# A fused encoder layer on one core: eight mixer weights split by GpSimd, square roots moved ahead of the last gate's output, and the K, V and Q projections moved in front of the pair jobs

## The chip, the core and the metric

The kernel runs on one NeuronCore of a Trainium2 chip. A core has five engines that run their own instruction queues in order and meet at semaphores: TensorE (PE in the profile; its weight loads are listed apart as PEld), VectorE (DVE), ScalarE (ACT), GpSimd (POOL) and SyncE (SP, which here only issues loads and stores). Operands lie in SBUF; matrix products come out in PSUM, in banks of 128 x 512 fp32. The metric is the device time of one execution in microseconds; the compared numbers are medians of several executions.

## What is computed

One layer of a hybrid encoder for 512 tokens and a model width of 1024, all in fp32: a SwiGLU feed-forward, a mixer, and a second feed-forward. The change lies in the mixer.

```python
u = rms_norm(h, mix_pre_g[l])
q, k, v, xr, xg = jnp.split(u @ w_in[l], splits, axis=-1)
xr = causal_conv(xr, conv_w[l], conv_b[l])
hr = rg_lru(xr, rg_a_w[l], rg_a_b[l], rg_x_w[l], rg_x_b[l], lru_lambda[l])
y_a = (hr * jax.nn.gelu(xg)) @ w_lru_out[l]
y_b = swa_sink_attention(q, k, v, attn_sinks[l], bias) @ w_attn_out[l]
g = jax.nn.sigmoid(u @ w_gate[l] + b_gate[l]).reshape(b, s, N_BRANCHES, d)
merged = g[:, :, 0] * y_a + g[:, :, 1] * y_b
h = h + rms_norm(merged @ w_o[l], mix_post_g[l])
```

`rg_lru` forms, for every channel, two sigmoid gates from small block products, a decay `a`, an input scaled by `sqrt(1 - a^2)`, and the scan `h[t] = a[t] * h[t-1] + input[t]` over the tokens.

## The kernel before, in words

**Split operands.** TensorE multiplies in fp32r, a shortened fp32. Every operand is therefore kept as two parts, a high part (the value copied to fp32r) and a low part (value minus high part), and a product is the sum of three matmuls: high weight by high input, low weight by high input, high weight by low input (lines 218 to 220 for plain units, 487 to 489 for pair jobs). A weight tile of 128 x 1024 is loaded raw by SyncE (`dma_one`, line 140, tile `raw_...`), its high part `whi` is a ScalarE copy (line 173) and its low part `wlo` a VectorE subtraction (line 174). For the keys in `BY_DMA` (line 1376) it goes another way, `split_dma` (line 152): ScalarE makes the high part and a negated copy of it, and an accumulating load issued by GpSimd adds the raw weight from memory to the negated copy. In the kernel before, these are the first four gate weights (`wg` 0 to 3) and, inside the pair jobs, the first split of every job but job 0.

**Units.** `unit(nm, i)` makes one 128-channel strip of a projection for all 512 tokens: 8 x 3 matmuls of 128 x 512 into one PSUM bank. `get` (line 178) hands out a unit's weight, emits the splits of the two weights that follow in the hand-written list `order` (line 96 on), and the raw loads of three more. A split stops at the indices in `paired`, the weights of pair jobs, which are prepared elsewhere.

**The hand-made order.** All engines' instructions are emitted in one program order and each queue keeps it. `later(n, fn, rank)` puts work `n` points ahead; `point()` counts up and emits what is due, lowest rank first. Each unit holds two points (after its 12th and 24th matmul) and each V product one; a pair job has one after each of its products. `point(True)` emits all that is outstanding.

**The mixer's stages before.** Relative to the start of the mixer's point count: four units of `xr` (points 1 to 8); eight units of `wg`, the gates of branch A (points 9 to 24); four V products (25 to 28); four pair jobs for `xg`; two K units; two Q units; then the eight output units of the recurrent branch (`lru`) mixed with the other Q units and the attention steps, and so on. Beside them run the convolution (`CONV_AT`), the recurrent gates (`RG_AT`), the decays (`DECAY_AT`: ScalarE exp and tanh, then three VectorE operations, lines 1047 to 1053), the square roots (`rg_scan`, line 1060, on ScalarE at the points of `SCAN_AT`) and, `SCAN_LAG` points later, the product and the scan on VectorE (lines 1063 and 1064). `gate_out` (line 1107) takes a gate's tanh out of its bank one point after its unit.

**Pair jobs.** `GeluPairs.run` makes `xg` by a fast 2 x 2 block scheme with seven products instead of eight. A job takes two raw weights; its operands are a11/a12 (first raw weight), the sums s1 to s4 (tiles `S`, made by GpSimd, lines 532 to 538) and a22. `prep(m, i)` prepares job m in five steps: 0, the four GpSimd sums; 1, the split of a11/a12; 2 and 3, the splits of the sums; 4, the split of a22. Within job n the steps 1 to 4 of job n+1 are emitted between the products, and at its end step 0 of job n+2 and the raw loads of job n+3. Job 0's steps and job 1's sums come earlier, at the points of `PREP_AT` and `PREP_1`. The seventh product of a job (a22) is made in the next job. After a job come the gelu (ScalarE), the product with the scan's result (line 686) and its split into `yh` and `yl`, the inputs of the `lru` units; four jobs give four pairs of these. The last job is followed by its own seventh product, product and split, and the first `lru` unit reads all four pairs.

**Buffers.** Nearly all SBUF tiles come from one pool of 42 slots of 4 KB a partition (`NSLOT`). A tile takes a slot when it is first used in program order, and its first writer waits until the slot's last reader is done; so SyncE's queue stops at a load whose slot is not yet free. `KS`, the split K of one KV head, fills four slots in all and `QS` one slot for each Q unit.

Of the kernel before, what the change touches and what calls it, by code (L numbers as in the profile page):

```python
# [15 lines left out]
P = 128  # L16
# [35 lines left out]
def hybrid_layer(ctx: ExitStack, tc: tile.TileContext, a: dict, out: bass.AP):  # L52
# [22 lines left out]
    def f32(ap):  # L75
        return ap.bitcast(F32)
# [41 lines left out]
    want("w2a", FT)  # L118
    order += [("xr", i) for i in range(8)]
    order += [("wg", i) for i in range(8)]  # L120
    order += [("wv", 0), ("wv", 1)]
    paired.update(range(len(order), len(order) + 8))
    order += [("xg", i) for i in range(8)]
    order += [("wk", 0), ("wk", 1), ("wq", 0), ("wq", 1)]

    att_units = [("lru", 0), ("wq", 2), ("wq", 3), ("lru", 1), ("wq", 4), ("wq", 5), ("lru", 2), ("lru", 3)]
    att_units += [("wq", 6), ("lru", 4), ("wq", 7), ("lru", 5), ("lru", 6), ("lru", 7)]
# [24 lines left out]
    def split_dma(r, src, shape=(P, D), hi=None):  # L152

        lo = slot(list(shape), F32R, name="wlo")
        if hi is None:
            hi = slot(list(shape), F32R, name="whi")
            act.activation(hi, r, AF.Copy)
        act.activation(lo, r, AF.Copy, scale=-1.0)
        pool.dma_start(out=lo, in_=src, accum_op=ALU.add)
        return hi, lo  # L160

    def split_to(n):
        while st["split"] < min(n, len(order)) and st["split"] not in paired:
            k = st["split"]
            dma_to(k + 1)
            r = raws.pop(k)
            if order[k] in BY_DMA:
                nm, i = order[k]
                pairs[k] = split_dma(r, a[nm][i * P : (i + 1) * P, :])
            else:  # L170
                hi = slot([P, D], F32R, name="whi")
                lo = slot([P, D], F32R, name="wlo")
                act.activation(hi, r, AF.Copy)
                dve.tensor_tensor(out=lo, in0=r, in1=f32(hi), op=ALU.subtract)
                pairs[k] = (hi, lo)
            st["split"] += 1

    def get(nm, i, ahead=2, rawahead=3):

        k = st["get"]  # L180
        assert order[k] == (nm, i), (order[k], nm, i)
        dma_to(k + 1 + ahead)
        split_to(k + 1 + ahead)
        dma_to(st["split"] + rawahead)
        st["get"] += 1
        return pairs.pop(k)
# [5 lines left out]
    def later(n, fn, rank=1):  # L192
        uid[0] += 1
        due.append((now[0] + n, rank, uid[0], fn))
# [297 lines left out]
    class Pairs:  # L492
# [14 lines left out]
        def prep(self, m, i, eng=None):  # L507
            if m >= len(self.jobs) or (m, i) in self.ready:
                return
            self.ready.add((m, i))  # L510
            k = self.k0 + 2 * m
            if i == 0:
                if k not in loaded or k + 1 not in loaded:
                    self.raws(m)
                s12, s34 = slot([P, 2 * QH], name="S12"), slot([P, 2 * QH], name="S34")
                self.w[m] = {"r": (raws.pop(k), raws.pop(k + 1)), "s": (s12, s34)}
            W = self.w[m]
            (ra, rb), (s12, s34) = W["r"], W["s"]
            a11, a12, a21, a22 = ra[:, :QH], ra[:, QH:], rb[:, :QH], rb[:, QH:]

            def both(src, w=2 * QH):
                hi = slot([P, w], F32R, name="whi")
                lo = slot([P, w], F32R, name="wlo")
                split2(hi, lo, src)
                return hi, lo

            def halves(p, a, b):
                W[a] = p[0][:, :QH], p[1][:, :QH]
                W[b] = p[0][:, QH:], p[1][:, QH:]

            def sums34(e):
                e.tensor_tensor(out=s34[:, QH:], in0=a12, in1=s12[:, QH:], op=ALU.subtract)
                e.tensor_tensor(out=s34[:, :QH], in0=a11, in1=a21, op=ALU.subtract)  # L533

            if i == 0:
                e = eng or pool
                e.tensor_tensor(out=s12[:, :QH], in0=a21, in1=a22, op=ALU.add)
                e.tensor_tensor(out=s12[:, QH:], in0=s12[:, :QH], in1=a11, op=ALU.subtract)
                if self.R is None:
                    sums34(e)  # L540
            elif i == 1:
                nm, t_ = order[k]
                p = split_dma(ra, a[nm][t_ * P : (t_ + 1) * P, :]) if nm in BY_DMA and m else both(ra)
                halves(p, "a11", "a12")
            elif i == 2:
                if self.R is not None:
                    sums34(dve)
                halves(both(s12), "s1", "s2")
            elif i == 3:
# [534 lines left out]
    for i, p in enumerate(PREP_AT):  # L1084
        later(p, lambda i=i: pairs_g.prep(0, i), 3)
    later(PREP_1, lambda: pairs_g.prep(1, 0), 3)


    lru, scans = {}, []
# [4 lines left out]
        later(p, lambda i=i: rg_gates(i))  # L1094
    for i in range(8):
        later(DECAY_AT[i], lambda i=i: rg_decay(i), 3)
        later(SCAN_AT[i], lambda i=i: rg_scan(i), 3)
    xr_ps = dict(enumerate(bs))
    for i in range(4, 8):
        xr_ps[i] = unit("xr", i)  # L1100
# [8 lines left out]
    for i in range(8):  # L1109
        ps = unit("wg", i)  # L1110
        later(1, lambda i=i, ps=ps: gate_out(i, ps))

    wv = [get("wv", i) for i in range(2)]
    V2 = [slot([P, 2, N_KV, 2, HD], F32R, name="V") for _ in range(2)]

# [14 lines left out]
        later(1, lambda t=t, o=o: v_out(t, o))  # L1130
        point()

    yh, yl = [], []
    pairs_g.run(scans, yh, yl, lambda: split_to(st["split"] + 1))
    X3 = pairs_g = None

    KS = {}

    def k_out(i, ps):
        ks = {r0: slot([P, 2, SEQ], F32R, name="KS") for r0 in (0, 64)}  # L1140
        for r0, k_ in ks.items():
            act.activation(k_[0:64, 0, :], ps[r0 : r0 + 64, :], AF.Copy)
            act.activation(k_[64:128, 0, :], ps[r0 : r0 + 64, :], AF.Copy)
        for r0, k_ in ks.items():
            dve.tensor_tensor(out=k_[r0 : r0 + 64, 1, :], in0=ps[r0 : r0 + 64, :], in1=f32(k_[r0 : r0 + 64, 0, :]), op=ALU.subtract)
        for r0, k_ in ks.items():
            o0 = 64 - r0
            act.activation(k_[o0 : o0 + 64, 1, :], f32(k_[r0 : r0 + 64, 1, :]), AF.Copy)
            KS[2 * i + r0 // 64] = k_

    for i in range(2):
        ps = unit("wk", i)
        later(1, lambda i=i, ps=ps: k_out(i, ps))
    QS = {}

    def q_out(i, ps):
# [8 lines left out]
    for i in range(2):  # L1165
        ps = unit("wq", i)
        later(1, lambda i=i, ps=ps: q_out(i, ps))

    def ya_out(i, ps):
        m = gz[i // 2][:, i % 2, :]  # L1170
# [194 lines left out]
ATT_LAG = (1, 1, 4, 1, 3, 1)  # L1365
RG_LAG = 2
DECAY_AT = (9, 10, 13, 14, 17, 18, 21, 22)
SCAN_AT = (25, 25, 25, 25, 26, 26, 26, 26)
SCAN_LAG = (1, 1, 2, 2, 2, 2, 3, 5)

T_AT = (3, 4, 5, 6), (4, 5, 6, 7)
PREP_AT = (19, 21, 23, 24, 25)
PREP_1 = 24
NSLOT = 42

BY_DMA = {("wg", i) for i in range(4)} | {"xg"}
RF = 7
RO = 6

# [58 lines left out]
```

## Time and profile before

| quantity | value |
|---|---|
| median of 3 runs | 1147.79 us (1144.2 to 1148.16) |
| profiled execution | 1145.55 us |
| its span on the core | 1142.8 us |
| mean granted TensorE clock | 0.994 |
| TensorE busy | 1122.5 us |
| VectorE busy | 823.7 us |
| ScalarE busy | 628.1 us |
| GpSimd busy | 353.7 us |
| bytes moved | 130.75 MB, mean 114 GB/s |

The span runs from the first to the last instruction of the core; the profiled execution's time is 2.75 us longer. The times of the rows count from the span's start. In the profile `c` is a PSUM bank of the pair jobs, `f` one of a unit, `v` one of V; `S` a tile of sums; `ct`, `cc` a job's results; `xc_t` the tile in which the recurrent branch keeps decay and root; `ig` the scan's tile. A row of instructions reads: start, length, engine, line, operation, output<-input, shape, count, and in brackets the idle time of the engine just before with what ended it. A row of a group reads: line, engine, operation, names and shapes, count, then busy time, mean ns of one, and idle time before. A row of waits reads: engine, line, what it waited for, total us, times, longest. Matmuls overlap, so a row's length is more than the distance to the next start; the distance is the rate.

### The profile page before, as it was taken

How to read it: one execution, taken by the hardware profiler on the slowest of the kernel's cores; microseconds unless marked ns; L12 is line 12 of the kernel's file. 1: busy time of each engine (PE TensorE's matmuls, PEld its weight loads, DVE VectorE, ACT ScalarE, POOL GpSimd, SP SyncE). 2: the span in 40 equal slices, each digit the busy share in tenths (PEclk: the TensorE clock that was granted, in tenths of full speed). 3: DMA queues.
4: the chain of work that ended last, by engine and by line, in shares of the span. 5: the costliest groups of instructions: out<-in, count | busy, mean ns of one | idle time of the engine just before them, and what ended most of it. 6: DMA issues, size and time to landing. Idle time of an engine off the chain costs nothing.

```text
span 1142.8 us, 17893 instructions
## 1 busy us (share of the span) xinstructions
PE 1122.5 (98%) x6973; PEld 1012.7 (89%) x6973; DVE 823.7 (72%) x1224; ACT 628.1 (55%) x1112; POOL 353.7 (31%) x274
## 2 busy tenths in 40 slices
PE   9999999999999999789999999999999999999997
PEld 7899999988889878788888888888999999998886
DVE  5889989796346968966678855767899777975313
ACT  7755565573246698466656653455555555574211
POOL 0043444200002404331466553000865566700000
PEclk9999999999999999899999999999999999999999
DMA  9226553364404651345122223431323332255101
GB/s 348 92 80 152 139 117 111 96 218 148 129 37 166 156 123 54 93 115 180 38 93 93 75 92 129 158 138 38 111 82 105 112 98 88 92 189 177 40 19 55
DMA packets 38725, 130.75 MB, mean 114 GB/s; under 512 B 4704, under 2 KB 6624, under 8 KB 38640
## 3 DMA queue, kind: packets, MB, share of 16 engines
q1 hardware_dynamic: 34128, 114.89, 30.1%
q0 software_dynamic: 4224, 14.20, 6.5%
q8 instruction: 54, 0.88, 0.3%
q10 hardware_dynamic: 288, 0.52, 0.1%
q14 instruction: 31, 0.25, 0.1%
HBM read 120.17 MB, written 7.33 MB: 112 GB/s over the span
## 4 chain that ended last, share of the span: by engine, by line
PE 55%; DMA 1%; DVE 0%; issue 0%; ACT 0%; DVEq 0%
PE c L488 6%; PE c L487 6%; PE c L489 6%; PE f L218 6%; PE f L220 6%; PE f L219 6%; PE acc L238 5%; PE acc L237 5%; PE acc L236 5%; PE pt L1235 1%; PE s L1199 1%; DMA wlo<-in_xg_dram 1%; PE s L1198 1%; PE o L1251 1%; PE o L1252 1%; PE tr L328 0%
## 5 line engine op out<-in xcount | busy, mean ns | idle before, releaser
L488 PE MATMUL c<-uT,wlo 128*128 128x256 f32 x504 | 143.5, 285 | 8.5 <-DMA wlo<-in_xg_dram 8.5
L218 PE MATMUL f<-uT,whi 128*128 128x512 f32 (+1 forms) x408 | 146.7, 360 | 0.0
L488 PE MATMUL c<-Xh,wlo 128*128 128x256 f32 x504 | 143.4, 285 | 2.8 <-DVE wlo L209 2.8
L219 PE MATMUL f<-uT,wlo 128*128 128x512 f32 (+1 forms) x408 | 145.3, 356 | 0.0
L220 PE MATMUL f<-uT,whi 128*128 128x512 f32 (+1 forms) x408 | 145.2, 356 | 0.0
L487 PE MATMUL c<-Xh,whi 128*128 128x256 f32 x504 | 143.2, 284 | 0.0
L489 PE MATMUL c<-uT,whi 128*128 128x256 f32 x504 | 143.2, 284 | 0.0
L487 PE MATMUL c<-uT,whi 128*128 128x256 f32 x504 | 143.0, 284 | 0.0
L236 PE MATMUL acc<-whi,hT 128*128 128x512 f32 x352 | 137.1, 390 | 0.0
L237 PE MATMUL acc<-wlo,hT 128*128 128x512 f32 x352 | 137.0, 389 | 0.0
L238 PE MATMUL acc<-whi,hT 128*128 128x512 f32 x352 | 136.9, 389 | 0.0
L489 PE MATMUL c<-Xl,whi 128*128 128x256 f32 x456 | 129.0, 283 | 0.0
L209 DVE TENSOR_TENSOR wlo<-S,whi 128x1024 fp32r<-128x1024 f32 x84 | 125.2, 1491 | 2.4 <-ACT whi L208 1.4
L488 PEld LDWEIGHTS c<-uT,wlo 128*128 128x128 f32 x504 | 97.3, 193 | 9.1 <-DMA wlo<-in_xg_dram 9.1
L488 PEld LDWEIGHTS c<-Xh,wlo 128*128 128x128 f32 x504 | 97.3, 193 | 3.2 <-DVE wlo L209 3.1
L208 ACT ACTIVATE whi<-S 128x1024 fp32r<-128x1024 f32 x84 | 86.1, 1054 | 22.0 <-DVE S L533 22.0
L487 PEld LDWEIGHTS c<-Xh,whi 128*128 128x128 f32 x504 | 97.3, 193 | 0.3 <-issue 0.3
L489 PEld LDWEIGHTS c<-uT,whi 128*128 128x128 f32 x504 | 97.3, 193 | 0.0
L487 PEld LDWEIGHTS c<-uT,whi 128*128 128x128 f32 x504 | 97.2, 193 | 0.0
L218 PEld LDWEIGHTS f<-uT,whi 128*128 128x128 f32 x408 | 77.1, 189 | 12.0 <-issue 1.4
L489 PEld LDWEIGHTS c<-Xl,whi 128*128 128x128 f32 x456 | 87.5, 192 | 0.0
L220 PEld LDWEIGHTS f<-uT,whi 128*128 128x128 f32 x408 | 77.1, 189 | 11.1
(352 smaller groups left out, 2832.6 us busy)
## 6 DMA issues: line engine op xcount, KB each, us to landing
raw_w2a<-in_w2a_dram SPq DMA_DIRECT2D x22, 512.0 KB, 4.2
raw_w1b<-in_w1b_dram SPq DMA_DIRECT2D x22, 512.0 KB, 4.2
raw_w3b<-in_w3b_dram SPq DMA_DIRECT2D x22, 512.0 KB, 4.2
raw_w2b<-in_w2b_dram SPq DMA_DIRECT2D x22, 512.0 KB, 4.1
raw_w3a<-in_w3a_dram SPq DMA_DIRECT2D x21, 512.0 KB, 4.6
raw_w1a<-in_w1a_dram SPq DMA_DIRECT2D x20, 512.0 KB, 4.4
raw_wg<-in_wg_dram SPq DMA_DIRECT2D x16, 512.0 KB, 4.0
raw_xr<-in_xr_dram SPq DMA_DIRECT2D x8, 512.0 KB, 4.0
```

The lines of the kernel that those rows point to most:

```text
L208: act.activation(hi, src, AF.Copy)
L209: dve.tensor_tensor(out=lo, in0=src, in1=f32(hi), op=ALU.subtract)
L218: pe.matmul(ps[:, c0:c1], wh[:, s], h_, start=k == 0, stop=False)
L219: pe.matmul(ps[:, c0:c1], wl[:, s], h_, start=False, stop=False)
L220: pe.matmul(ps[:, c0:c1], wh[:, s], l_, start=False, stop=k == KT - 1)
L236: pe.matmul(acc[n], x[:, 0, c], wh[:, s], start=first, stop=False)
L237: pe.matmul(acc[n], x[:, 0, c], wl[:, s], start=False, stop=False)
L238: pe.matmul(acc[n], x[:, 1, c], wh[:, s], start=False, stop=last)
L487: pe.matmul(ps, wh[:, s], xh, start=first, stop=False, skip_group_check=True)
L488: pe.matmul(ps, wl[:, s], xh, start=False, stop=False, skip_group_check=True)
L489: pe.matmul(ps, wh[:, s], xl, start=False, stop=k == 3, skip_group_check=True)
L1198: pe.matmul(o, lq, KS[g][:, 0, k0 : k0 + n], start=True, stop=False)
```

## The change

It does four things, in one edit.

1. The list `order` has K ahead of V, and V and Q ahead of `xg`; the code of the K and Q units stands ahead of `pairs_g.run`, with one `point(True)` between. The points are then: gates 9 to 24, K 25 to 28, V 29 to 32, Q 33 to 36, then the pair jobs, then `lru` 0.
2. The new set `BY_POOL` names `wg` 2 to 7 and both K weights: their high part is a GpSimd `tensor_copy` in place of the ScalarE copy; the low part is the VectorE subtraction. `BY_DMA` keeps `wg` 0 and 1 alone, and the pair jobs' step 1 always splits with a ScalarE copy and a VectorE subtraction.
3. All eight square roots are emitted at point 23 (rank 4, the last of what is due there), which is ahead of the last gate's tanh at point 25; the scans follow one by one at points 24 to 31.
4. The first two raw weights of the pair jobs are loaded at point 18 and the next two at point 27 (`RAW_AT`); job 0's steps move to points 22, 27, 29, 31 and 33, job 1's sums to point 30.

```diff
     order += [("wg", i) for i in range(8)]
-    order += [("wv", 0), ("wv", 1)]
+    order += [("wk", 0), ("wk", 1), ("wv", 0), ("wv", 1)]
+    order += [("wq", 0), ("wq", 1)]
     paired.update(range(len(order), len(order) + 8))
     order += [("xg", i) for i in range(8)]
-    order += [("wk", 0), ("wk", 1), ("wq", 0), ("wq", 1)]
...
-                act.activation(hi, r, AF.Copy)
+                if order[k] in BY_POOL:
+                    pool.tensor_copy(hi, r)
+                else:
+                    act.activation(hi, r, AF.Copy)
                 dve.tensor_tensor(out=lo, in0=r, in1=f32(hi), op=ALU.subtract)
...
             elif i == 1:
-                nm, t_ = order[k]
-                p = split_dma(ra, a[nm][t_ * P : (t_ + 1) * P, :]) if nm in BY_DMA and m else both(ra)
-                halves(p, "a11", "a12")
+                halves(both(ra), "a11", "a12")
...
     later(PREP_1, lambda: pairs_g.prep(1, 0), 3)
+    for n, p in enumerate(RAW_AT):
+        later(p, lambda n=n: [dma_one(pairs_g.k0 + 2 * n + j) for j in range(2)], 3)
...
-        later(SCAN_AT[i], lambda i=i: rg_scan(i), 3)
+        later(SCAN_AT[i], lambda i=i: rg_scan(i), 4)
...
-SCAN_AT = (25, 25, 25, 25, 26, 26, 26, 26)
-SCAN_LAG = (1, 1, 2, 2, 2, 2, 3, 5)
+SCAN_AT = (23,) * 8
+SCAN_LAG = (1, 2, 3, 4, 5, 6, 7, 8)
...
-PREP_AT = (19, 21, 23, 24, 25)
-PREP_1 = 24
+RAW_AT = (18, 27)
+PREP_AT = (22, 27, 29, 31, 33)
+PREP_1 = 30
...
-BY_DMA = {("wg", i) for i in range(4)} | {"xg"}
+BY_DMA = {("wg", i) for i in range(2)}
+
+BY_POOL = {("wg", i) for i in range(2, 8)} | {("wk", 0), ("wk", 1)}
```

The functions `k_out` (a K strip out of its bank into two `KS` tiles: four ScalarE copies, two VectorE subtractions, two more ScalarE copies) and `q_out` (two ScalarE copies, two VectorE operations) are moved as they are.

More of the change, by code (lines that the diff above doesn't have):

```diff
@@ L1111, in hybrid_layer, with k_out @@
         later(1, lambda i=i, ps=ps: gate_out(i, ps))
+    KS = {}
+    def k_out(i, ps):
+        ks = {r0: slot([P, 2, SEQ], F32R, name="KS") for r0 in (0, 64)}
+        for r0, k_ in ks.items():
+            act.activation(k_[0:64, 0, :], ps[r0 : r0 + 64, :], AF.Copy)
+            act.activation(k_[64:128, 0, :], ps[r0 : r0 + 64, :], AF.Copy)
+        for r0, k_ in ks.items():
+            dve.tensor_tensor(out=k_[r0 : r0 + 64, 1, :], in0=ps[r0 : r0 + 64, :], in1=f32(k_[r0 : r0 + 64, 0, :]), op=ALU.subtract)
+        for r0, k_ in ks.items():
+            o0 = 64 - r0
+            act.activation(k_[o0 : o0 + 64, 1, :], f32(k_[r0 : r0 + 64, 1, :]), AF.Copy)
+            KS[2 * i + r0 // 64] = k_
+    for i in range(2):
+        ps = unit("wk", i)
+        later(1, lambda i=i, ps=ps: k_out(i, ps))
     wv = [get("wv", i) for i in range(2)]
@@ L1131, in hybrid_layer @@
         point()
[L1133 to L1153, printed above, removed]
     QS = {}
@@ L1167, in hybrid_layer @@
         later(1, lambda i=i, ps=ps: q_out(i, ps))
+    yh, yl = [], []
+    point(True)
+    pairs_g.run(scans, yh, yl, lambda: split_to(st["split"] + 1))
+    X3 = pairs_g = None
     def ya_out(i, ps):
```

## The prediction

> **What bounds the kernel now.** The page's head and first part come first, then the waits of TensorE (line waited for, total, times, longest).
>
> ```profile
> span 1142.8 us, 17893 instructions
> ...
> PE 1122.5 (98%) x6973; PEld 1012.7 (89%) x6973; DVE 823.7 (72%) x1224; ACT 628.1 (55%) x1112; POOL 353.7 (31%) x274
> ```
>
> ```profile
> PE c L488 <- DMA wlo<-in_xg_dram: 8.5, 3, 4.0
> PE c L488 <- DVE wlo L209: 2.8, 1, 2.8
> PE w L722 <- DVE tiny L728: 1.4, 1, 1.4
> PE c L487 <- ACT ct L672: 0.5, 1, 0.5
> ```
>
> TensorE sets the end: it is busy for 98%, and apart from the start its only waits, 8.5 + 2.8 + 0.5 = 11.8 us, all carry the name c, the banks of the pair jobs. The next two views are busy times by stretch (the columns after the length are PE, PEld, DVE, ACT, POOL, then granted clock and DMA), and TensorE's own order of time.
>
> ```profile
> 402.00:450.87 48.87, 48.87 (x230) 38.88 (x229) 37.08 (x50) 47.50 (x65) 8.64 (x6) 1.00 0.40 94
> 450.87:462.59 11.72, 11.72 (x99) 11.68 (x97) 11.61 (x11) 8.20 (x15) 6.54 (x4) 1.00 0.05 4
> 462.59:518.56 55.97, 44.28 (x339) 43.18 (x338) 42.94 (x44) 29.34 (x48) 17.64 (x11) 0.91 0.48 130
> 470.00:480.00 10.00, 4.44 (x25) 3.94 (x23) 9.90 (x8) 0.50 (x2) 6.26 (x4) 0.70 0.55 152
> ```
>
> ```profile
> 450.62 0.39 PE L219 MATMUL f<-uT,wlo 128*128 128x512 f32 x1
> 450.85 0.39 PE L220 MATMUL f<-uT,whi 128*128 128x512 f32 x1
> ...
> 462.59 0.28 PE L487 MATMUL c<-uT,whi 128*128 128x256 f32 x1
> 462.71 0.28 PE L488 MATMUL c<-uT,wlo 128*128 128x256 f32 x1
> ...
> 475.55 0.58 PE L488 MATMUL c<-uT,wlo 128*128 128x256 f32 x1 [4.04 <-DMA wlo<-in_xg_dram]
> 475.92 0.41 PE L489 MATMUL c<-uT,whi 128*128 128x256 f32 x1
> 476.14 0.41 PE L487 MATMUL c<-uT,whi 128*128 128x256 f32 x1
> ...
> 518.40 0.40 PE L218 MATMUL f<-uT,whi 128*128 128x512 f32 x1
> ```
>
> Pair matmuls start every 0.12 us, but after the 4.04 us wait every 0.21 us, while the granted clock of that stretch reads 0.70. The four jobs hold 28 products of 12 matmuls: 336 x 0.12 = 40.3 us. They take 518.40 - 462.59 = 55.8 us. So **15.5 us** are lost here, 11.8 as waits and about 3.7 to the slower clock and restarts. That is the most that can be won; before and after this stretch TensorE has no gap. A 128x512 matmul takes 0.23 us, so a unit of 24 takes 5.5 us.
>
> **The parts.** *High and low parts of the pair weights.* For jobs 1 to 3 the low part of a11/a12 is now made by ScalarE (a negated copy) and an accumulating load issued by GpSimd.
>
> ```profile
> 468.24 0.88 POOL L159 DMA_DIRECT2D wlo<-in_xg_dram  x1 [10.45 <-ACT ct L660]
> ```
>
> ```profile
> raw_xg<-in_xg_dram SPq DMA_DIRECT2D x8, 512.0 KB, 3.6
> ...
> wlo<-in_xg_dram POOLq DMA_DIRECT2D x3, 512.0 KB, 7.3
> ```
>
> Job 0's seventh product comes only in job 1, so it lasts 6 x 12 x 0.12 = 8.6 us, and this load, issued 5.6 us into it, lands 7.3 us later: 4.3 us past the start of job 1, which is the wait seen. The change makes the low part by one subtraction on VectorE after the same high-part copy. The 8.5 us go, and since the code has no such load for xg any more, that part cannot fail to happen; VectorE gains 3 x 1.22 us (row L174 below), ScalarE loses three copies.
>
> *The copies.*
>
> ```profile
> L208 ACT ACTIVATE whi<-S 128x1024 fp32r<-128x1024 f32 x84 | 86.1, 1054 | 22.0 <-DVE S L533 22.0
> ```
>
> ```profile
> 366.54 12.46 POOL L1080 TENSOR_TENSOR xf<-xf,xf 128x1024 f32<-128x1024 f32 x4 [11.81 <-ACT xf L345]
> ...
> 431.19 2.17 POOL L537 TENSOR_TENSOR S<-raw_xg 128x512 f32<-128x512 f32 x1 [17.99 <-DMA raw_xg<-in_xg_dram]
> ...
> 563.36 4.20 POOL L1219 TENSOR_SCALAR P<-P,d 128x256 f32<-128x256 f32 x4 [3.56 <-PE s L1199]
> ```
>
> Six gate weights and both K weights get their high part from GpSimd. Two of the gate weights lose the negated copy and load too: ScalarE, busy for 47.50 of 48.87 us in the gate stage, sheds eight 128x1024 passes. A GpSimd copy of 128x1024 is in no row. The bounds: 1.05 us as on ScalarE; 4.2 us from four 128x256 one-input operations. The nearest row by size and kind, 12.46 / 4 = 3.1 us for a two-input one, is the value I take. Even 4.2 is below the 5.5 us of a unit, so the copies keep up with TensorE and cost it nothing. If that fails, the subtraction behind a late copy stops VectorE's queue, the decays and scans in it too: the price is rival B's. The wait that they add stands before the second K weight, whose copy is queued behind job 0's four sums: these began at 431.2, after 18 us for their load; four of about 2.2, the copy 3.1 and the subtraction 1.2 make 444, and K's second unit starts at 451 + 5.5 = 456. What a GpSimd operation does to VectorE:
>
> ```profile
> 373.31 3.42 DVE L983 TENSOR_TENSOR rglo<-rgraw,rghi 128x1024 fp32r<-128x1024 f32 x1
> 386.68 1.22 DVE L174 TENSOR_TENSOR wlo<-raw_xr,whi 128x1024 fp32r<-128x1024 f32 x1
> 563.74 1.23 DVE L174 TENSOR_TENSOR wlo<-raw_wq,whi 128x1024 fp32r<-128x1024 f32 x1 [0.57 <-ACT whi L173]
> ```
>
> Beside a two-input GpSimd operation the same subtraction takes 3.42 instead of 1.22 us, 2.2 more; beside one-input ones it takes 1.23, nothing more. A copy has one input, so I take 0, and keep 2.2 us per copy as the other end (no row shows one that gains). [...]
>
> *Order of the stage.* K, V and Q stand before the jobs; their four K and Q units (4 x 5.5 = 22 us) used to come after. TensorE's work is the same; the jobs start 22 us later relative to the gates, and the first recurrent-output unit (lru 0) follows them directly. VectorE's load in the new stretch, gates' end to jobs' start, 11.7 + 22 = 33.7 us:
>
> ```profile
> 460.07 0.68 DVE L1063 TENSOR_TENSOR ig<-xc_t,ig 128x512 f32<-128x512 f32 x1
> 460.78 1.23 DVE L1064 TENSOR_TENSOR_SCAN ig<-xc_t,ig 128x512 f32<-128x512 f32 x1
> ```
>
> ```profile
> L174 DVE TENSOR_TENSOR wlo<-raw_wq,whi 128x1024 fp32r<-128x1024 f32 x8 | 9.7, 1222 | 3.5 <-ACT whi L173 3.5
> L1162 DVE SCALAR_TENSOR_TENSOR QS<-f,QS 64x512 fp32r<-64x512 f32 x16 | 11.0, 688 | 3.2 <-ACT QS L1160 3.0
> L209 DVE TENSOR_TENSOR V<-v,V 128x256 fp32r<-128x256 f32 x4 | 1.6, 404 | 0.0
> ```
>
> Eight scans with their products 8 x 1.9 = 15.3; four V and Q weight splits 4.9; K and Q 8 x 0.69 = 5.5, V 1.6; job 0's splits 3.5 x 1.22 = 4.3; together 31.7. The four GpSimd sums of job 1, 128x512, half as long as the row above, add half of 2.2 each, 4.4: **36.1 of 33.7 us**, so VectorE comes about 2.4 us late to the jobs. The gate stage before keeps its balance (in: two gate and two K splits; out: two V and two job splits; 37.08 of 48.87 busy), and its 11.8 us to spare would take in most of the copies' worst case. Job 0 wants its first subtraction about 4.3 us after its start (third copy out, then the high part 1.05) and must have it done at 8.6: a delay up to 8.6 - 1.2 = 7.4 us is free. The second stall, 2.8 us for a VectorE low part behind the scans, goes as well.
>
> ScalarE's moved copies, twelve for K and four for Q,
>
> ```profile
> 524.06 0.59 ACT L1142 ACTIVATE KS<-f 64x512 fp32r<-64x512 f32 x1 [0.33 <-PE f L220]
> ```
>
> are 16 x 0.6 = 9.6 us in a stretch of 33.7. In SyncE's queue the four loads of K and Q pass the last four of xg, whose first four get fixed places; at 3.6 us each, two a job of 10.1 us are hidden unless slots are missing (rival C).
>
> In the jobs VectorE has 3 x 3.5 x 1.22 = 12.8 for splits, 4 x 1.2 = 5 for sums (three of 0.41 in a job, by the V row), 8 x 1.22 = 9.8 for products and low parts of y, 2.4 for two later weights, and eight GpSimd sums at 1.1: 38.8 us beside 40.3. It just fits, with no room: I give it **1.5 us** of waits (0 to 6).
>
> *Square roots first.* Now they stand late, with a table load of their own:
>
> ```profile
> 455.07 1.28 ACT L1060 ACT_TABLE_LOAD   x1
> ```
>
> All eight move ahead of the last gate's tanh, which then wants its table back: one more 1.28 us, covered, since ScalarE has shed 8 x 1.05 in the gate stage. Uncovered it would be 1.28 us.
>
> *The end of the jobs.* The K and Q units that covered the last job's y are gone, so y is late next:
>
> ```profile
> 519.52 1.22 DVE L686 TENSOR_TENSOR cc<-cc,ig 128x1024 f32<-128x1024 f32 x1
> 521.86 1.23 DVE L209 TENSOR_TENSOR yl<-cc,yh 128x1024 fp32r<-128x1024 f32 x1 [1.13 <-ACT yh L208]
> ```
>
> It is there at 523.1, 4.7 us after the jobs' last matmul (518.4). lru 0 needs it for its 21st matmul, 20 x 0.23 = 4.6 us in: a wait of 0.1 us if VectorE is on time, up to 5 if it is a few us late; I take **0.5**. With the 0.5 us behind ct, which stays, the sum is 15.5 - 0.5 - 0.5 - 1.5 = 13.0 us. The profiled execution took 1145.55 us (its span and 2.75): 1132.6. The median of the runs shown, 1147.79, lies 2.2 higher, which gives 1134.8; I write **1134**.
>
> **Rivals.** *A, forecast*: 1129 to 1139, the full 15.5 on the profiled time up to 9 on the median's.
>
> *B, VectorE becomes the bound.* Each copy blocks it for 2.2 us: 17.6, of which the gate stage takes 11.8; it is 5.8 + 2.4 = 8.2 us late at the jobs, and with 38.8 us of work beside 40.3 it is still 6.7 late at their end: as much waiting, and 3.7 if one wait, like the 4.04, drops the clock. 15.5 - 0.5 - 6.7 - 3.7 leaves 4.6 won: 1143, or 1139.5 without the clock (both on the median). For it: VectorE was busy 9.90 of 10 us beside the stalls. Against: the row at 563.74.
>
> *C, slower: buffers.* K and Q keep six of the 42 slots through the jobs. SyncE's queue of loads waits for slots even now (from 340 to 560 us):
>
> ```profile
> SPq L144 <- PE f L220: 58.4, 5, 16.3
> SPq L144 <- PE c L489: 36.3, 7, 12.9
> ```
>
> By the code, job 1 of the changed kernel holds all 42 when its next split is made. If a job's slots only come free as the job before ends, jobs 2 and 3 start with a chain of their own: load 3.6, two GpSimd sums of half of 3.1, high part 1.05, low part 1.22, together 9.0 us, and 3.7 us of clock each: 25 us against the 13 won, 1158 on the profiled time and 1160 on the median. It decides once a slot is more than about 8 us late. Against: weights are asked for a job or more ahead, and the longest such waits went by without a gap in TensorE.
>
> *D, cover lost at lru 0.* VectorE is 5 us late there: 15.5 - 0.5 - 1.5 - 5 - 3.7 = 4.8 won, 1143 on the median. For it: nothing stands between the jobs and lru 0 any more. Against: the sum of 38.8 fits.
>
> **Chances.** A 0.58, B 0.15, C 0.17, D 0.10. This kernel's measurement tells 0.5% (5.7 us) from no change: faster is below 1142.1, slower above 1153.5. Faster: A, half of B and half of D, 0.70. Slower: most of C, 0.15. Same: 0.15. The range runs from 1128 (all won, on the fastest run) to 1150, which leaves out C's slow part; A's own is 1129 to 1139.
>
> **What would show it.** Right: no wait for a load of xg, granted clock 1.00 through the jobs, last job matmul about 41 to 43 us after the first, a second table load at L1107, VectorE's subtractions beside GpSimd copies at 1.23. Wrong: subtractions of 2 to 3.4 us beside copies (B); TensorE waiting in the jobs for GpSimd sums or raw loads (C); a wait at the first lru unit for yl (D). A GpSimd copy over 5.5 us would overturn the whole first stage.

## The result and the profile after

| quantity | before | after |
|---|---|---|
| median | 1146.34 us (5 runs, 1144.2 to 1148.16) | 1129.70 us (5 runs, 1129.42 to 1131.82) |
| profiled execution | 1145.55 us | 1129.63 us |
| its span | 1142.8 us | 1127.8 us |
| mean granted clock | 0.994 | 0.999 |

The changed kernel takes 0.9856 of the time before, with a 95% interval of 0.984 to 0.9873: 16.6 us faster on the medians, 15.0 us in the span.

The head of the changed kernel's page, and all that TensorE waits for in its trace (line waited for, total, times, longest):

```profile
span 1127.8 us, 17899 instructions
...
PE 1118.9 (99%) x6973; PEld 1010.0 (90%) x6973; DVE 828.4 (73%) x1229; ACT 617.5 (55%) x1100; POOL 356.3 (32%) x277
```

```profile
PE w L723 <- DVE tiny L729: 1.4, 1, 1.4
PE c L490 <- ACT ct L673: 0.5, 1, 0.5
PE f L772 <- ACT uT L765: 0.2, 1, 0.2
```

The 8.5 and 2.8 us of waits on the banks `c` are gone; the 0.5 us behind ScalarE's last copy stays. Three stretches of the changed kernel, with the same columns as before: the gate stage, the K, V and Q units, and the four pair jobs.

```profile
402.00:450.50 48.50, 48.50 (x227) 38.58 (x226) 42.87 (x56) 39.68 (x58) 11.97 (x9) 1.00 0.32 96
```

```profile
450.00:484.50 34.50, 34.50 (x199) 30.51 (x198) 29.39 (x35) 21.61 (x33) 6.11 (x4) 1.00 0.14 45
484.50:525.30 40.80, 40.33 (x336) 40.12 (x334) 33.57 (x35) 27.43 (x46) 15.63 (x11) 1.00 0.35 109
```

The jobs now take 41.0 us, from 484.5 to the first matmul behind them at 525.54 (its row stands with experiment 10; the stretch above ends 0.2 us earlier), where they took 55.8. Their 336 matmuls need 40.3 at 0.12 us each. The granted clock is 1.00 in all three. The 14.8 us between the two are nearly the whole change of the span, 15.0 us: next to nothing was won or lost elsewhere. VectorE, busy for 9.90 of 10 us beside the old stalls, has 7.2 us to spare in the jobs, and ScalarE, which was full in the gate stage, has 8.8 us to spare there.

The new parts, in order of time. First GpSimd's copies (with three of its four sums left out), then the VectorE instructions that stand beside copies and two later ones, then ScalarE's table load:

```profile
396.35 3.34 POOL L174 CAST whi<-raw_wg 128x1024 fp32r<-128x1024 f32 x3
407.70 1.05 POOL L174 CAST whi<-raw_wg 128x1024 fp32r<-128x1024 f32 x1 [8.01 <-PE f L222]
...
436.98 1.28 POOL L540 TENSOR_TENSOR S<-raw_xg 128x512 f32<-128x512 f32 x1 [2.76 <-PE r L1037]
...
443.04 1.50 POOL L174 CAST whi<-raw_wk 128x1024 fp32r<-128x1024 f32 x1
...
469.87 1.28 POOL L540 TENSOR_TENSOR S<-raw_xg 128x512 f32<-128x512 f32 x1 [25.33 <-DVE wlo L177]
```

```profile
396.75 3.24 DVE L1011 CAST xcs<-xc_t 128x512 fp32r<-128x512 f32 x1
...
412.40 0.42 DVE L1011 CAST xcs<-xc_t 128x512 fp32r<-128x512 f32 x1
...
443.57 2.06 DVE L177 TENSOR_TENSOR wlo<-raw_wk,whi 128x1024 fp32r<-128x1024 f32 x1
...
447.40 1.22 DVE L177 TENSOR_TENSOR wlo<-raw_wk,whi 128x1024 fp32r<-128x1024 f32 x1
...
473.42 1.57 DVE L212 TENSOR_TENSOR wlo<-S,whi 128x1024 fp32r<-128x1024 f32 x1 [0.66 <-ACT whi L211]
474.91 1.78 DVE L1064 TENSOR_TENSOR ig<-xc_t,ig 128x512 f32<-128x512 f32 x1
...
482.21 1.23 DVE L1065 TENSOR_TENSOR_SCAN ig<-xc_t,ig 128x512 f32<-128x512 f32 x1
...
484.38 1.39 DVE L1161 SCALAR_TENSOR_TENSOR QS<-f,QS 64x512 fp32r<-64x512 f32 x2
...
488.94 1.23 DVE L212 TENSOR_TENSOR wlo<-raw_xg,whi 128x1024 fp32r<-128x1024 f32 x1 [1.61 <-ACT whi L211]
...
528.94 1.22 DVE L212 TENSOR_TENSOR yl<-cc,yh 128x1024 fp32r<-128x1024 f32 x1 [1.13 <-ACT yh L211]
```

```profile
453.45 1.28 ACT L1110 ACT_TABLE_LOAD   x1
```

Four things are to be seen. A GpSimd copy of 128x1024 takes 1.04 to 1.5 us. It does delay VectorE: the first K weight's subtraction (443.57), beside the copy of the second K weight (443.04 to 444.54), takes 2.06 instead of 1.22 us, and a cast that met three copies 3.24 instead of 0.42. (The two rows at 473.42 and 474.91 are used further down.) The last scan ends at 483.4, 1.1 us before the first pair job, so VectorE comes to the job's first subtraction (488.94) early and waits 1.61 us for ScalarE. And the second table load falls where it was forecast, ahead of the last gate's tanh, where ScalarE has room.

### The profile page after: what moved, and what is told of

The parts are those of the page before. It is cut to its first block, busy times and chain, and to the rows that moved or that the text cites. A ratio compares the mean times of both kernels' runs of the same rounds, so it can differ in the third digit from the quotient of the medians.

```text
span 1127.8 us, 17899 instructions
## 1 busy us (share of the span) xinstructions
PE 1118.9 (99%) x6973; PEld 1010.0 (90%) x6973; DVE 828.4 (73%) x1229; ACT 617.5 (55%) x1100; POOL 356.3 (32%) x277
## 4 chain that ended last, share of the span: by engine, by line
PE 99%; DMA 0%; DVE 0%; issue 0%; ACT 0%; DVEq 0%; SPq 0%
PE c L490 13%; PE c L492 13%; PE c L491 13%; PE f L221 10%; PE f L222 10%; PE f L223 10%; PE acc L239 8%; PE acc L240 8%; PE acc L241 8%; PE pt L1239 1%; PE s L1203 1%; PE s L1202 1%; PE tr L331 1%; PE o L1255 1%; PE o L1256 1%; PE f L772 1%
```

## The experiments

**The question.** The prediction gives the gain to the accumulating loads (8.5 us of waits), to the low part behind the scans (2.8 us) and to the clock; the order of the units is there as cover, the copies and the early roots as means to bring VectorE and ScalarE in on time. The rival view is that one part carries nearly all of it and the rest is idle. Each part was undone by itself, and the parts were added to the kernel before. All ratios are to the kernel before on the same chip.

**1. The accumulating loads back in the pair jobs** (all else as changed).

```diff
-BY_DMA = {("wg", i) for i in range(2)}
+BY_DMA = {("wg", i) for i in range(2)} | {"xg"}
...
-                halves(both(ra), "a11", "a12")
+                nm, t_ = order[k]
+                p = split_dma(ra, a[nm][t_ * P : (t_ + 1) * P, :]) if nm in BY_DMA and m else both(ra)
+                halves(p, "a11", "a12")
```

> The changed kernel with one part undone: for jobs 1 to 3 the low part of a11/a12 comes from GpSimd's accumulating load again. Theory 1 (two causes: the load comes too late by its own length, and VectorE is late from the scans; the order cures only the second): the load is asked for 5.4 to 5.6 us into a job and takes 7.3, so it is 4.3 us late for job 1 and about 2.6 for jobs 2 and 3, 9.5 us of waits, and 3.7 for the clock after the first: 1129.7 + 13 = 1142 us (1139 to 1144), three waits named after the load and none for a VectorE low part. Rival (with K, V and Q in front there is time enough for the loads too, and the order alone won everything): 1130 to 1132.

Measured: 1137.54 us, ratio 0.9925 (0.9908 to 0.9941). TensorE's waits in the jobs, then the matmul behind the longest of them with the two that follow, and then two of the stretches behind it (granted clock after POOL's column):

```profile
PE c L491 <- DMA wlo<-in_xg_dram: 4.6, 3, 2.5
```

```profile
495.92 0.39 PE L491 MATMUL c<-uT,wlo 128*128 128x256 f32 x1 [2.49 <-DMA wlo<-in_xg_dram]
496.14 0.28 PE L492 MATMUL c<-uT,whi 128*128 128x256 f32 x1
496.26 0.28 PE L490 MATMUL c<-uT,whi 128*128 128x256 f32 x1
```

```profile
496.00:498.00 2.00, 2.00 (x15) 2.00 (x16) 2.00 (x2) 0.57 (x2) 2.00 (x2) 0.86 0.87 336
498.00:500.00 2.00, 2.00 (x11) 2.00 (x10) 0.78 (x1) 0.00 (x0) 0.23 (x1) 0.50 0.03 10
```

Against the changed kernel's 1129.70 us the loads cost about 8 us, between what the two views said. The waits return, but as 4.6 us, not 8.5, and with a short spell at half clock. So the mechanism was there and its size was not that of the kernel before: the first load is issued as far into job 0 as there (at 490.15, 5.6 us after the job's start), but these loads land in 5.6 us instead of 7.3.

**2. The accumulating loads taken out of the kernel before, and nothing else.**

```diff
-BY_DMA = {("wg", i) for i in range(4)} | {"xg"}
+BY_DMA = {("wg", i) for i in range(4)}
```

> The kernel before with the accumulating loads of xg taken out and nothing else: the low part of a11/a12 of jobs 1 to 3 is a VectorE subtraction. Theory 1: the subtraction stands behind the scans, which kept VectorE busy until 480 us, so job 1 waits about 10 us (from 471.2 to 481) in place of 4.0 and 2.8, the clock drops as before, the later waits go: 1143 to 1147, against 1146.3 before. Rival (the 8.5 us of waits named after the load are simply won, and the clock with them): 1134 to 1138.

Measured: 1140.46 us, ratio 0.995 (0.9933 to 0.9967): 5.7 us won, where 8.5 us of waits and the clock hung on these loads. TensorE's waits say why, and VectorE's queue ahead of the instruction that it waits for:

```profile
PE c L488 <- DVE wlo L209: 7.3, 1, 7.3
```

```profile
475.31 1.68 DVE L1063 TENSOR_TENSOR ig<-xc_t,ig 128x512 f32<-128x512 f32 x1
477.03 1.22 DVE L1064 TENSOR_TENSOR_SCAN ig<-xc_t,ig 128x512 f32<-128x512 f32 x1
478.17 1.20 DVE L209 TENSOR_TENSOR wlo<-raw_xg,whi 128x1024 fp32r<-128x1024 f32 x1
```

All three waits for a load are gone, and one wait of 7.3 us stands in place of the first and of the 2.8 us behind it. The low part that the load used to make is now VectorE's, and VectorE reaches it at 478.17, behind the scans; job 1 had been waiting for it since about 472. In the kernel before the two delays lay over each other: with the first gone, the second was there.

**3. All of the change except the order of K, V and Q and the pair jobs.** With the order go the points that belong to it: those of the pair jobs' first loads and steps (part 4 of the change). The code that moves with the order is left out of the diff.

```diff
-    order += [("wk", 0), ("wk", 1), ("wv", 0), ("wv", 1)]
-    order += [("wq", 0), ("wq", 1)]
+    order += [("wv", 0), ("wv", 1)]
...
     order += [("xg", i) for i in range(8)]
+    order += [("wk", 0), ("wk", 1), ("wq", 0), ("wq", 1)]
...
-RAW_AT = (18, 27)
-PREP_AT = (22, 27, 29, 31, 33)
-PREP_1 = 30
+PREP_AT = (19, 21, 23, 24, 25)
+PREP_1 = 24
```

> The changed kernel with the order of the stages put back (V, pair jobs, K, Q; job 0's steps at the old points); the loads stay out, the GpSimd copies and the early square roots stay in. Theory 1: VectorE has 15.3 us of scans, 4.3 of splits, 1.6 of V and 4.4 of delay by GpSimd sums between 450 and the jobs' start at 462.6; job 1's first low part is 3 to 6 us late, and the clock drops once: 1129.7 + 4 to 10 = 1134 to 1140. Rival (with the roots early and ScalarE relieved, the scans are done in time in any order): 1129 to 1131.

Measured: 1139.91 us, ratio 0.9948 (0.9933 to 0.9963). The wait is that of experiment 2, to 0.1 us:

```profile
PE c L491 <- DVE wlo L212: 7.4, 1, 7.4
```

So in the old order neither the copies nor the early roots bring the scans out of the way; the order (with its points) does, and it is worth about 10 us in the changed kernel.

**4. Loads out and new order, without the copies and the early roots** (all eight high parts by ScalarE, the first four gate weights by the accumulating load as before).

```diff
-SCAN_AT = (23,) * 8
+SCAN_AT = (25,) * 8
-BY_DMA = {("wg", i) for i in range(2)}
+BY_DMA = {("wg", i) for i in range(4)}
-BY_POOL = {("wg", i) for i in range(2, 8)} | {("wk", 0), ("wk", 1)}
+BY_POOL = set()
```

> The loads out and the new order, but no GpSimd copies (ScalarE makes the eight high parts; gate weights 0 to 3 by negated copy and load as before) and the square roots two points later, behind the last gate's tanh. Theory 1 (these two parts only give slack): 1130 to 1132, no wait over 1 us. Rival (ScalarE, busy for 47.5 of 48.9 us in the gate stage, holds the whole chain back, and the copies are what counts): waits for ScalarE or VectorE at K, V or job 1 of 4 us or more, 1135 to 1142.

Measured: 1133.87 us, ratio 0.9894 (0.9879 to 0.9909), between the two. Some 4 us of the gain hang on the copies or the roots and their scans. The next two runs part them.

**5. The copies back to ScalarE, the roots early.**

```diff
-BY_POOL = {("wg", i) for i in range(2, 8)} | {("wk", 0), ("wk", 1)}
+BY_POOL = set()
```

> The changed kernel, with ScalarE instead of GpSimd making the high parts of the six gate and two K weights; the loads stay out, the order and the early square roots stay. Leaving out the copies and the early roots together (and giving two weights their accumulating load back) cost 4.2 us against the changed kernel. Theory 'roots': the early roots carry that, through scans that end earlier and a VectorE that is on time at the first pair job. Then this run lies at 1130 to 1131 us, with no wait of TensorE over 0.5 us in the pair jobs that the changed kernel does not have. Theory 'copies': ScalarE, full in the gate stage again, hands everything on late: 1133 to 1135 us, with waits for ct and wlo in the first two pair jobs.

Measured: 1129.83 us, ratio 0.9859 (0.9844 to 0.9874), not to be told from the changed kernel. The gate stage of this run, and its page's busy times:

```profile
402.00:450.50 48.50, 48.50 (x227) 38.58 (x226) 38.76 (x52) 45.43 (x62) 6.24 (x4) 1.00 0.33 96
```

```profile
PE 1118.4 (99%) x6973; PEld 1009.6 (90%) x6973; DVE 823.2 (73%) x1229; ACT 625.3 (55%) x1108; POOL 348.0 (31%) x269
```

Against the changed kernel's row above, ScalarE does 5.8 us more and VectorE 4.1 us less (5.2 us less in the whole kernel: 823.2 against 828.4). Both fit in the 48.5 us, and TensorE misses neither. The last scan ends at 485.3 instead of 483.4, which is still in time. The copies on GpSimd cost no time and win none here.

**6. The roots late, the copies on GpSimd.**

```diff
-SCAN_AT = (23,) * 8
+SCAN_AT = (25,) * 8
```

> The changed kernel, with the square roots and scans behind the last gate's output again; copies, loads and order as in the changed kernel. Theory 'roots': the scans end some 6 us later, VectorE comes late to the second pair job's low parts, and the time is 1133 to 1134 us, with waits for wlo or ct. Theory 'copies': 1130 to 1131 us, one table load less and no new wait.

Measured: 1133.03 us, ratio 0.9887 (0.9872 to 0.9902): 3.2 us more than experiment 5 on the same chip, so the early roots carry what was missing, together with their scans: these now follow at points 26 to 33, two later than in the changed kernel. Late roots with scans as close together as in the kernel before (points 26 to 31) were not tried. TensorE's waits in the jobs, VectorE's last scan and what follows it, and ScalarE's first copy in the jobs:

```profile
PE c L490 <- ACT ct L655: 1.5, 2, 0.8
...
PE c L491 <- DVE wlo L212: 0.9, 1, 0.9
```

```profile
489.15 1.23 DVE L1065 TENSOR_TENSOR_SCAN ig<-xc_t,ig 128x512 f32<-128x512 f32 x1
490.41 2.80 DVE L1161 SCALAR_TENSOR_TENSOR QS<-f,QS 64x512 fp32r<-64x512 f32 x4
493.24 2.19 DVE L212 TENSOR_TENSOR wlo<-raw_xg,whi 128x1024 fp32r<-128x1024 f32 x1
```

```profile
488.03 0.39 ACT L655 ACTIVATE ct<-c 128x256 f32<-128x256 f32 x1 [1.95 <-DVE ig L1065]
```

The scans end at 490.4 instead of 483.4, and the first low part is done at 495.4 instead of 490.2. That is past the start of job 1, and it costs 0.9 us. The other 1.5 us are two waits of 0.8 us for `ct`. Ahead of the first, ScalarE itself waits 1.95 us for a scan before it may write `ct`, a tile that takes nothing from the scan, so by the code it waits for the slot of a tile that the scan is the last to read. It is rival C's mechanism, at 0.8 us. The second, 0.79 us ahead of the matmul at 510.81, comes in job 2; what held ScalarE there is not shown.

**7. The order alone, on the kernel before.**

```diff
-SCAN_AT = (23,) * 8
+SCAN_AT = (25,) * 8
...
-BY_DMA = {("wg", i) for i in range(2)}
-BY_POOL = {("wg", i) for i in range(2, 8)} | {("wk", 0), ("wk", 1)}
+BY_DMA = {("wg", i) for i in range(4)} | {"xg"}
+BY_POOL = set()
```

with the lines of experiment 1 that split by load. The diff is against the changed kernel, so part 4 of the change, the new points of the pair jobs' loads and steps, is in this kernel too, and the scans follow the late roots at points 26 to 33, where the kernel before has them at 26 to 31.

> The kernel before, with only the order of K, V and Q and the pair jobs changed: the accumulating loads are there, ScalarE makes all high parts, the roots stand late. If the parts add (the changed kernel with the loads back cost 7.8 us, without copies and early roots 4.2 us): 1129.7 + 12 = 1141.7 us, 1140 to 1143. Rival, both delays overlap since the low parts come late one way or the other: 1137.5 to 1139.5 us. In both the 7 us wait for a low part behind the scans is gone, which the kernel with the loads alone taken out still has.

Measured: 1135.59 us, ratio 0.991 (0.9893 to 0.9927). Both guesses were too high: the order with its points wins 10.1 us, more than any other part.

TensorE's waits in the jobs, the median time from issue to landing of the accumulating loads, and the stretch of the jobs:

```profile
PE c L491 <- DMA wlo<-in_xg_dram: 4.0, 3, 1.9
...
PE c L490 <- ACT ct L657: 0.8, 1, 0.8
```

```profile
wlo<-in_xg_dram POOLq DMA_DIRECT2D x3, 512.0 KB, 5.5
```

```profile
484.50:530.40 45.90, 40.62 (x330) 39.57 (x329) 35.23 (x38) 29.46 (x49) 16.09 (x13) 1.00 0.52 135
```

The low part behind the scans is not waited for any more (2.8 us), the loads land in 5.5 us instead of 7.3, so their waits halve (4.5 us), and the clock holds: it reads 1.00 over the jobs (about 3.7 us by the prediction's estimate); 0.8 us behind `ct` are new. Together these make about 10 us. Why the loads land sooner was not tried, so it is open how much of this another kernel would see. This kernel is no slower than that of experiment 1 (1137.54 us), which has the copies and the early roots besides but the one wait of 2.49 us; that it is faster by 2 us the two intervals do not prove.

**8. Each GpSimd copy made twice.**

```diff
                     pool.tensor_copy(hi, r)
+                    pool.tensor_copy(hi, r)
```

> The changed kernel, where each of the eight GpSimd copies is made twice. In the changed kernel's trace a copy takes 1.04 to 1.5 us and the VectorE operation beside it 0.65 to 0.86 us more. Theory: eight further copies cost VectorE about 8 x 0.75 = 6 us in the gate stage, which has that to spare, so TensorE shows no new wait: 1129 to 1131 us. Rival B of the prediction, VectorE is already at its limit: it comes about 6 us late to the jobs, and the time goes to 1134 us or more with waits for wlo in the pair jobs.

Measured: 1130.21 us, ratio 0.9862 (0.9847 to 0.9877), with no wait that the changed kernel does not have. The page's busy times:

```profile
PE 1119.5 (99%) x6973; PEld 1010.3 (90%) x6973; DVE 831.9 (74%) x1229; ACT 617.8 (55%) x1100; POOL 366.2 (32%) x285
```

Eight copies more make VectorE busy for 3.5 us more, 0.44 us a copy: less than the 0.75 us expected. Not every copy meets an instruction that it delays: the one at 407.70 in the changed kernel runs beside three operations of the convolution that take 2.31 us, as they do elsewhere in that trace. VectorE is not at its limit in this stage.

**9 and 10. y made late at the end of the jobs**, by two and by six more VectorE passes over the last job's result.

```diff
             mult()
+            for _ in range(2):
+                dve.tensor_copy(c, c)
             parts()
```

> The changed kernel, with two more passes of VectorE over the last pair job's result (each a copy of 128x1024 onto itself; estimate from the 128x512 cast of 0.42 us: 0.8 us each) ahead of the split of y. Theory, the prediction's step on the end of the jobs: y is ready just in time, so nearly all of the 1.6 us becomes a wait of TensorE at lru 0 and the clock holds: 1131 to 1132 us. Rival: the products of the attention that stand between the matmuls of lru 0 cover it: 1129.5 to 1130.3 us, no such wait.

> The changed kernel with six such passes, some 4.8 us. Theory: a wait of about 4.5 us at lru 0, and a clock of about half speed for some us behind it, as behind the 4.04 us wait of the kernel before: 1136 to 1139 us (case D of the prediction gave 5 us for the wait and 3.7 us for the clock). Rival: the wait alone, since the matmuls that follow are of another kind or the clock holds: 1133.5 to 1135 us.

Measured: 1130.73 us, ratio 0.9866 (0.9851 to 0.988), and 1135.09 us, ratio 0.9904 (0.9889 to 0.9918). The passes take 1.42 and 4.40 us. The matmul of lru 0 that waits in the first, and in the second the longer of its two waits with the two stretches behind it:

```profile
531.68 0.50 PE L223 MATMUL f<-yl,whi 128*128 128x512 f32 x1 [0.53 <-DVE yl L212]
```

```profile
PE f L221 <- ACT yh L211: 2.7, 1, 2.7
```

```profile
536.00:538.00 2.00, 2.00 (x7) 1.51 (x6) 1.51 (x11) 0.52 (x4) 0.61 (x2) 0.51 0.09 33
538.00:540.00 2.00, 2.00 (x7) 1.60 (x6) 0.34 (x2) 2.00 (x9) 0.10 (x1) 0.64 0.00 0
```

In the changed kernel y is there at 530.16 (528.94 + 1.22), and the matmul that wants it starts at 531.04 (the first row is the first matmul behind the jobs):

```profile
525.54 0.40 PE L221 MATMUL f<-yh,whi 128*128 128x512 f32 x1
...
528.29 0.22 PE L1202 MATMUL s<-KS,QS 128*128 128x128 f32 x1
...
529.13 0.45 PE L221 MATMUL f<-yh,whi 128*128 128x512 f32 x1
...
531.04 0.40 PE L223 MATMUL f<-yl,whi 128*128 128x512 f32 x1
```

Eight small products of the attention stand between the matmuls of lru 0, from 528.29 to 529.13. They are 0.8 us of cover that the prediction did not see; y has 0.9 us to spare. Both runs lie between their two guesses. With y 1.42 us late the wait is 0.53 us, which is 1.42 less the 0.9 to spare; the median is 1.0 us above the changed kernel's, and the intervals leave the rest open. With y 4.40 us late the cost is 5.4 us: two waits of 3.2 us together, and some 3 us at about half clock behind them.

**11. The early roots alone, on the kernel before.**

```diff
-        later(SCAN_AT[i], lambda i=i: rg_scan(i), 3)
+        later(SCAN_AT[i], lambda i=i: rg_scan(i), 4)
...
-SCAN_AT = (25, 25, 25, 25, 26, 26, 26, 26)
-SCAN_LAG = (1, 1, 2, 2, 2, 2, 3, 5)
+SCAN_AT = (23,) * 8
+SCAN_LAG = (1, 2, 3, 4, 5, 6, 7, 8)
```

> The kernel before, with the square roots and scans ahead of the last gate's output and nothing else. With the new order the early roots are worth 3.3 us. Theory: they are worth that only there; in the old order the scans are not done before the second job's low parts either, and ScalarE, full in the gate stage, has the second table load to pay: 1145 to 1148 us. Rival: the low part that waits behind the scans comes earlier here too: 1142 to 1144 us.

Measured: 1145.88 us, ratio 1.0004 (0.9994 to 1.0013). Nothing, as the theory had it: the waits are 7.6 us for loads and 2.0 us for the low part behind the scans.

**12. One wait less in the last job.** The changed kernel's 0.5 us behind `ct` comes from the last job alone, where the product that adds to a bank follows at once on the copy out of it.

```diff
-                mm_s(W["a12"], X["b21"], bc)
-                dve.tensor_tensor(out=c[:, 0, :256], in0=bc, in1=q1, op=ALU.add)
+                def c11():
+                    mm_s(W["a12"], X["b21"], bc)
+                    dve.tensor_tensor(out=c[:, 0, :256], in0=bc, in1=q1, op=ALU.add)
+
+                if n < end:
+                    c11()
...
                 dve.tensor_tensor(out=c[:, 1, 256:], in0=v, in1=q5, op=ALU.add)
+                if n == end:
+                    c11()
                 gelu(c[:, 0, :])
```

> The changed kernel, where in the last pair job alone the product a12 times b21 stands behind s3 times t3 instead of ahead of s4 times b22, so that 12 matmuls lie between the copy out of the accumulator and the last product that adds to it. The changed kernel still waits 0.47 us there, and its y is ready 0.9 us before it is needed. Theory: the wait goes and y stays in time: 1128.9 to 1129.4 us. Rival: the sum behind a12 and the activation that needs it come about 1.4 us later and y is late by what was won: 1129.5 to 1130.3 us, with a wait for yh or yl at lru 0.

Measured: 1129.27 us, ratio 0.9858 (0.984 to 0.9875). The wait is gone, and what is left of TensorE's waits is the one at the start of the program:

```profile
PE w L730 <- DVE tiny L736: 1.4, 1, 1.4
```

The span is 1127.6 us, 0.2 less than the changed kernel's, though the wait was 0.5. The jobs end 0.7 us sooner (524.88), but y is there 0.4 us later (530.54), and the matmul that reads it starts some 0.2 us late. Its ratio can't be told from the changed kernel's, so it is no proven gain.

**What they come to.** Against the kernel before, in us (each by the medians on its own chip):

| parts made | won | last limit in the jobs |
|---|---|---|
| early roots | none | loads, low part behind the scans |
| loads out | 5.7 | low part behind the scans, 7.3 |
| order, with its points | 10.1 | loads, 4.0 |
| loads out, copies, early roots | 6.3 | low part behind the scans, 7.4 |
| order, copies, early roots | 8.7 | loads, 4.6, and the clock |
| loads out, order | 12.3 | VectorE late by the scans |
| loads out, order, copies | 12.7 | the same |
| loads out, order, early roots | 15.9 | 0.5 |
| all | 16.6 | 0.5 |

The parts don't add. Job 1's first low part had two things late at once, a load and VectorE's queue; either cure alone leaves the other, and when both are gone the scans are next, which is where the early roots pay.

## Why the prediction was right, and where it was not

**The total.** The 15.5 us lost in the jobs were the right measure: 14.8 of them were won, and 0.5 us stayed behind `ct` as foreseen. The forecast of 1134 us is 4.3 us too high. 2.0 us, by the span, are the two waits that it took, 1.5 in the jobs and 0.5 at lru 0, which did not come. 0.9 us lie around the span, 1.8 us after against 2.75 before. 1.4 us are what the forecast put on top of its own sum, 1132.6, for the three-run median; five runs of before have their median at 1146.34, only 0.8 us over the profiled execution.

**The loads.** "The 8.5 us go, and since the code has no such load for xg any more, that part cannot fail to happen": the waits for the loads went, the time did not go with them. This is the step that failed as it was put. Without the new order 5.7 us came of it, since a wait of 7.3 us for VectorE took the place. The sum was right because the order was in it too, and the second stall, which "goes as well", was counted as a separate 2.8 us; it was what was left of VectorE's delay once the wait for the load had covered the first part of it. So the total was forecast from the right loss, and the shares of the parts were not.

**The order.** It was treated as cover and as VectorE's load, and given no gain of its own. It is the largest part: 10.1 us alone, with the points that go with it.

**VectorE ahead of the jobs.** 36.1 of 33.7 us were forecast, 2.4 us late (the terms of the 31.7 in it add up to 31.6, which changes nothing); measured are 29.39 of 34.50, and VectorE was early. Two terms were off by most of the difference. The four Q operations (2.8 us, from 484.38 on) fall practically behind the start of the jobs, and GpSimd's sums of job 1 delayed VectorE by some 1.5 us, not 4.4: 1.57 instead of 1.22 us at 473.42 and 1.78 instead of 0.68 at 474.91. The free delay of 7.4 us was not touched. Its bound shows in experiment 6: the scans end 6.9 us later than in the changed kernel, the first low part of job 1 starts 8.7 us after the jobs' start, and the wait for it is 0.9 us.

**The copies.** 3.1 us each was taken, 1.04 to 1.5 was measured; the lower bound, ScalarE's 1.05, was the nearest. That they keep up with a unit of 5.5 us held. The second K weight's copy was done at 444.5 and its subtraction at 448.6 (447.40 + 1.22), where the forecast had 444 for the subtraction; 456 would have been in time. Experiment 5 shows that the copies neither cost nor won time.

**Their price on VectorE.** The choice of 0 was wrong. VectorE is busy for 5.2 us more than in experiment 5, 0.65 us for each of the eight copies, and eight copies more cost 3.5 us in experiment 8, 0.44 us each; the subtraction at 443.57 lost 0.84 us to one copy, and the cast at 396.75 lost 2.8 us to three. Why the row at 563.74, on which the choice rested, shows no delay stays open. Rival B had the mechanism, with 2.2 us a copy more than three times the size; its sign, a subtraction of 2 to 3.4 us beside a copy, was seen (2.06), its loss of time was not. That the wrong price did no harm is due to the room in the gate stage, where VectorE is still idle for 5.6 of 48.5 us.

**The jobs.** 38.8 of 40.3 us were forecast for VectorE (38.6 with 4 x 1.2 as 4.8), 33.57 of 40.80 measured. There is room, and the 1.5 us of waits was too careful.

**The end of the jobs.** The row at 518.40, which the prediction calls the jobs' last matmul, is the first one behind them. From that matmul on (525.54 in the changed kernel) y was forecast after 4.7 us and came after 4.6. The need was put at 4.6 us; with the attention's eight products it is 5.5. Case D, had VectorE been 5 us late, would have cost about what experiment 10 shows, 5.4 us for 4.4.

**Rival C.** K and Q hold their slots, and waits for slots are there: the GpSimd sums of job 1 start 25.33 us after the engine was free, released by a subtraction for a Q weight, from which they take nothing; by the code that is a wait for a slot. None reached TensorE in the changed kernel. In experiment 6 a slot that comes free late costs 0.8 us, not a chain of 9. With fewer slots it was not tried.

## What to carry to other kernels

When a critical instruction is late for two reasons, the profile names only the one that ended last; ask where its other operands come from and when they would have been there, because the cure of one reason is worth no more than the distance to the other. Moving work that needs nothing late (here the K, V and Q units) in front of the work that does can be worth more than taking the late operand's slow maker away: 10.1 against 5.7 us here. And an engine's relief counts only where that engine is waited for: 5.8 us off a ScalarE that was busy for 45.4 of 48.5 us changed nothing.

## What the hardware showed beside this

**The clock does not follow from the length of a wait alone.** In experiment 1 a wait of 2.49 us was followed, some 1.5 us after TensorE had started again, by about 3 us at half clock (0.50 in the stretch 498 to 500). In the kernel before, a longer one was not:

```profile
506.18 0.39 PE L488 MATMUL c<-uT,wlo 128*128 128x256 f32 x1 [2.77 <-DMA wlo<-in_xg_dram]
...
508.08 0.28 PE L488 MATMUL c<-Xh,wlo 128*128 128x256 f32 x1
508.20 0.28 PE L489 MATMUL c<-wlo,whi 128*128 128x256 f32 x1
```

Two microseconds later the matmuls still start 0.12 us apart, and the granted clock reads 1.00 in every 2 us from 504 to 516. In the pair jobs waits of up to 1.9 us (experiment 7, clock 1.00) lost no clock in any run shown here; 2.49 us did (0.50) and 2.77 us did not, 2.72 us with 0.53 us behind it did at lru 0 (experiment 10, 0.51), and 4.04 us did (0.50 from 474 to 478 in the kernel before). What decides between them the runs do not show.

**A GpSimd copy is as fast as ScalarE's** at this size: 1.05 us at 407.70 in the changed kernel, against 1.054 us. The two-input sums on the same engine take at least 1.28 us (436.98) for half as many elements.
